# Another order of the attention's pieces in a list-scheduled decoder layer

## The chip, the core and the metric

The kernel runs on one core of a Trainium2 chip. The metric is the device time of one execution in microseconds (us), the median of three runs: 1217.39 us (1216.54, 1217.39 and 1219.12). One further execution was taken with the hardware profiler on. Engines are called PE (TensorE, the matrix products), PEld (its weight loads), DVE (VectorE), ACT (ScalarE), POOL (GpSimd) and SP (SyncE, which here only issues transfers).

## The reference

One layer of a decoder on a prompt of 1024 tokens and, beside it, 8 samples of one token each, with the same weights; the model is 1024 wide. All 1032 tokens go through the same products as columns.

```python
x = x + jnp.concatenate([ya, yb], axis=-1) @ w_out      # pooling and convolution mixers
x = x + cross_attn(rmsnorm(x, g_attn), mk, mv, w_q, w_o)
x = x + (jax.nn.silu(h @ w_gate) * (h @ w_up)) @ w_down # h = rmsnorm(x, g_ffn)

def cross_attn(h, k, v, w_q, w_o):                      # 4 heads of 256, 256 memory tokens
    q = (h @ w_q).reshape(B, L, MEM_HEADS, MEM_HEAD_DIM)
    s = jnp.einsum('blhd,bmhd->bhlm', q, k).astype(jnp.float32) / math.sqrt(MEM_HEAD_DIM)
    p = jax.nn.softmax(s, axis=-1).astype(v.dtype)
    o = jnp.einsum('bhlm,bmhd->blhd', p, v).reshape(B, L, D_MODEL)
    return o @ w_o
```

The prompt attends to one memory, whose keys and values (k, v) are computed here and shared by all its 1024 tokens. Each of the 8 samples has its own cached keys and values (2 MB of keys and 2 MB of values per head, for all samples), so its scores and values are not matrix products for PE; they are computed on DVE.

## The kernel before

Activations lie transposed: 128 channels on the partitions, tokens in the free dimension. A product of full precision is made of three passes over numbers split in two parts (high by high, high by low, low by high). A group of outputs, 128 channels by 1032 tokens, takes 72 matmuls of 344 columns (three spans, eight blocks of input, three passes). ACT copies a result to its high part, DVE subtracts to get the low part; that pair is called a drain here, and it frees the PSUM buffer that PE wants for a later group.

The attention is made of pieces, each a small function that adds tasks:

- `q` (`q_group`, line 1012): the queries of 128 channels, named `qo0` to `qo7`; two of them make a head. Their weights `w_q` come in two parts. For some groups the low part is made by DVE (line 384), for others ACT prepares it and a transfer from the POOL queue adds to it (line 402); which group of the order gets which is fixed by its place in the order.
- `S` (`scores`, line 1019): scores of a head for 256 tokens, 12 matmuls into `sc`, the maxima on DVE (1044), the exponentials on ACT (1053), the normalisation on DVE or POOL (1061). Pieces 0 to 3 are head 0, and so on; `sc3_1` is head 3, piece 1.
- `T` (`p_transpose`, line 1065): four transposes of the probabilities into `pt`, drained into `pT`.
- `P` (`pv`, line 1083): the values' products of 128 channels of a head, two halves of 512 tokens with 6 matmuls each, into `pv`, drained into `oo` by ACT (1098) and DVE (1099). Pieces 6 and 7 are head 3.
- For the samples of head h: `a` turns the queries into rows and writes them to memory (`qd`); `b` reads them back broadcast over the partitions (`sbcache_k`), loads the cached keys (`spcache_k`) and multiplies and sums on DVE (line 1133), four samples or eight at a time; `c` is their softmax (`ss`, `sst`, `prow`), written to `pd`; `d` does with the values (`sbcache_v`, `spcache_v`) what `b` did with the keys; `e` (POOL, lines 375 and 384) splits the result into the sample columns of `oo`.
- `o` (`proj_o`, line 1194): a group of the output product, `po`, over all `oo`. For `o0` and `o4` the columns with the samples come last. Its x (`x1d`) is loaded into `xa`, the sum is written to `x2d`. The pieces from `x` on (lines 1231 to 1247 are theirs) prepare the feed-forward part.

The table `ORDER` (line 41) lists the pieces; lines 1618 and 1619 run through it. That does not fix the order of instructions by itself: it numbers the tasks. `Program.order` (line 146) then plays the tasks through with costs written down in the kernel and picks for each engine the task that can start first, within a small slack the one with the lowest number. Buffers have slots: `pv`, `ps` and `po` share two (of three PSUM banks each), small tiles like `pt`, `ss` and most `sc` share two of one bank, the samples' cache tiles share three or, where eight samples go at once, lie among the operands' slots. A task whose buffer has no free slot waits. An engine executes its instructions in the order that comes out, and so does each queue of transfers, SP's and POOL's.

Of the kernel before, what the change touches and what calls it, by code (L numbers as in the profile page):

```python
# [40 lines left out]
ORDER = (  # L41
# [5 lines left out]
)  # L47

# [27 lines left out]
A12, A22, S4, S1, A11, S2, S3 = range(7)  # L76
# [1786 lines left out]
```

## Time and profile before

| | us |
|---|---|
| median of three runs | 1217.39 |
| lowest, highest | 1216.54, 1219.12 |
| the profiled execution's own time | 1217.88 |
| its span in the profile | 1216.1 |
| PE busy in it | 1198.4 |
| last query group's products end, the next scores begin | 409.78 |
| first output product (`po`) begins | 447.82 |

A row of the timeline reads: start, length, engine, line, operation, output and inputs by name, how often; in brackets how long the engine was idle before it, and on which instruction it waited. Names in the profile have lost their numbers, so `pv` is any of the eight. PE's lengths overlap, since the next matmuls start while the last ones run out. A row of the windows names, for a stretch of the span, the busy time and instruction count of each engine, the granted clock of PE (1.00 is full speed), the share of time that the transfer engines were busy, and their rate. In an answer on one tile, "DMA to landing" is the time from the issue of its transfers until a semaphore tells that they have landed, for those where the trace shows it.

### The profile page before, as it was taken

Reading aid. Unit: us, or ns where it says so; the run is one execution under the profiler, and the core shown is the slowest. Engines: PE = TensorE matmul, PEld = TensorE weight load, DVE = VectorE, ACT = ScalarE, POOL = GpSimd, SP = SyncE. Lnnn points to the kernel's source line nnn. Section 1 sums busy time; section 2 is a strip of 40 time slices with the busy share of each in tenths; the row PEclk is TensorE's granted clock in tenths of the full one; section 3 lists DMA queues with packets and bytes.
Section 4 is the critical chain, followed back from the end, with each engine's and each line's share of the span. In section 5 each row is a group of like instructions: output and inputs, shape, how many; then the busy total and the mean of one; then the engine's idle time right before and its main releaser. Section 6 shows DMA issues by size and latency. Waiting matters only on the chain.

```text
span 1216.1 us, 19401 instructions
## 1 busy us (share of the span) xinstructions
PE 1198.4 (99%) x7720; PEld 1121.8 (92%) x7720; DVE 930.1 (76%) x1548; ACT 524.7 (43%) x718; POOL 251.4 (21%) x297
## 2 busy tenths in 40 slices
PE   8999999999999999999999999999999999999997
PEld 7999988999999979999999999999999999999886
DVE  7999999766258886679877777777867798879744
ACT  7765656455135533454222322233222355544633
POOL 3568842231111102131000000000000024332101
PEclk9999999999999999999999999999999999999999
DMA  7335677326386774422332233222313597678612
GB/s 289 86 73 116 144 210 223 117 104 207 108 266 205 244 271 150 122 87 66 118 114 80 96 114 111 108 79 97 123 70 105 206 309 216 169 195 222 150 52 89
DMA packets 60170, 179.69 MB, mean 148 GB/s; under 512 B 7792, under 2 KB 11568, under 8 KB 58800
## 3 DMA queue, kind: packets, MB, share of 16 engines
q1 hardware_dynamic: 53824, 157.92, 37.4%
q0 software_dynamic: 6256, 20.54, 9.9%
q8 instruction: 60, 0.98, 0.3%
q14 instruction: 30, 0.25, 0.1%
HBM read 144.66 MB, written 33.78 MB: 147 GB/s over the span
## 4 chain that ended last, share of the span: by engine, by line
PE 78%; DVE 4%; DMA 1%; issue 1%; ACT 1%; POOL 0%; DVEq 0%; SPq 0%; ACTq 0%
PE pr L1339 48%; PE po L485 8%; PE fd L1682 6%; PE ps L485 5%; PE oa L485 4%; PE ob L485 4%; PE sc L1036 1%; DVE spcache_k L1133 1%; PE pv L1094 1%; DMA sbcache_v<-pd 1%; DVE oo L1099 1%; PE kps L860 0%; DVE pT L1080 0%; DMA raw<-in_w_k 0%; DMA pd<-prow 0%
## 5 line engine op out<-in xcount | busy, mean ns | idle before, releaser
L1339 PEld LDWEIGHTS pr<-ab,wTb 128*128 128x128 f32 x1056 | 131.8, 188 | 3.5
L1339 PE MATMUL pr<-ab,wTa 128*128 128x260 f32 x1056 | 133.6, 282 | 0.2 <-DVE su L1355 0.2
L1339 PE MATMUL pr<-ab,wTb 128*128 128x260 f32 x1056 | 133.0, 282 | 0.0
L1339 PEld LDWEIGHTS pr<-ab,wTa 128*128 128x128 f32 x1056 | 130.8, 188 | 2.4 <-DVE su L1355 0.4
L1339 PE MATMUL pr<-ab,wG 128*128 128x512 f32 x528 | 129.3, 393 | 0.0
L1355 DVE TENSOR_TENSOR su<-pr,su 128x520 f32<-128x520 f32 (+1 forms) x112 | 77.7, 695 | 57.9 <-PE pr L1339 57.7
L1339 PEld LDWEIGHTS pr<-ab,wG 128*128 128x128 f32 x528 | 96.3, 188 | 19.7 <-DVE wG L384 0.4
L485 PE MATMUL ps<-xop,w 128*128 128x344 f32 x720 | 114.1, 320 | 0.0
L485 PEld LDWEIGHTS ps<-xop,w 128*128 128x128 f32 x720 | 113.6, 188 | 0.0
L1339 PEld LDWEIGHTS pr<-hb,dV 128*128 128x128 f32 x768 | 98.8, 188 | 4.1
L1339 PE MATMUL pr<-hb,dV 128*128 128x260 f32 x768 | 100.1, 283 | 0.0
L485 PE MATMUL ps<-xq,w 128*128 128x344 f32 x576 | 94.9, 322 | 0.5 <-DMA w<-in_w_q 0.5
L485 PEld LDWEIGHTS ps<-xq,w 128*128 128x128 f32 x576 | 90.8, 188 | 0.9 <-DMA w<-in_w_q 0.8
L485 PEld LDWEIGHTS po<-oo,w 128*128 128x128 f32 x576 | 90.8, 188 | 0.6 <-DVE oo L1099 0.4
L485 PE MATMUL po<-oo,w 128*128 128x344 f32 x576 | 91.3, 320 | 0.0
L694 DVE SCALAR_TENSOR_TENSOR cacc<-glu,vec,cacc 128x511 f32<-128x511 f32 (+14 forms) x116 | 76.9, 744 | 0.0
L1339 PE MATMUL pr<-hb,dW 128*128 128x512 f32 x288 | 74.6, 394 | 0.0
L373 ACT ACTIVATE w<-raw 128x1024 fp32r<-128x1024 f32 (+1 forms) x37 | 34.9, 949 | 86.1 <-PE po L485 24.2
L1682 PE MATMUL fd<-ho,w 128*128 128x260 f32 (+1 forms) x432 | 69.1, 321 | 0.0
L1366 POOL MEMSET su<- 128x16 f32 x22 | 2.5, 112 | 318.9 <-PE pr L1339 267.7
L1682 PEld LDWEIGHTS fd<-ho,w 128*128 128x128 f32 x432 | 62.0, 188 | 6.9 <-issue 0.5
L1339 PE MATMUL pr<-ab,wU 128*128 128x512 f32 x264 | 64.6, 393 | 0.0
(309 smaller groups left out, 2189.2 us busy)
## 6 DMA issues: line engine op xcount, KB each, us to landing
gr<-in_w_gu SPq DMA_DIRECT2D x44, 512.0 KB, 3.7
hb<-su SPq DMA_DIRECT2D x8, 1040.0 KB, 4.6
hs<-hb SPq DMA_DIRECT2D x16, 520.0 KB, 5.1
dr<-in_w_dn SPq DMA_DIRECT2D x16, 512.0 KB, 4.6
spcache_k<-in_cache_k SPq DMA_DIRECT2D x12, 512.0 KB, 5.1
hs<-hb SPq DMA_DIRECT2D x12, 512.0 KB, 5.0
raw<-in_w_in SPq DMA_DIRECT2D x10, 512.0 KB, 3.7
hb<-he SPq DMA_DIRECT2D x8, 520.0 KB, 3.6
```

The costliest lines, as they stand in the source:

```text
L373: e.activation(dst(0), src(), AF.Copy, scale=1.0 if gain is None else gain)
L485: e.matmul(ps[:, c, :CW], w[:, wi, cols], x[:, xi, c * CW : (c + 1) * CW], start=first and p == 0, stop=last and p == 2)
L694: e.scalar_tensor_tensor(acc[h][:, n:], src[:, : HALF - n], w, acc[h][:, n:], ALU.mult, ALU.add)
L1036: e.matmul(bank()[:, i * NMEM : (i + 1) * NMEM], qop[2 * h + dt][:, qi, tt * P : (tt + 1) * P], kk[:, ki, 2 * (h % 2) + dt], start=(dt == ...
L1094: e.matmul(ps[:, c], v[:, vi, m, col : col + P], pT[h][m][:, pi, sl], start=(m == 0 and p == 0), stop=(m == 1 and p == 2))
L1099: add({"DVE": dve(512)}, lambda e, c=c, sl=sl: e.tensor_tensor(oo[:, 1, sl], ps[:, c], f32(oo[:, 0, sl]), ALU.subtract), [(ps, c), (oo, 0, ...
L1133: e.scalar_tensor_tensor(piece[:, b], piece[:, b], 1.0, bc[:, b], ALU.mult, ALU.mult, accum_out=out(m)[:, first + b : first + b + 1])
L1339: e.matmul(bank(c), w[:, wi, cols(j)], xs[0](j, xi)[:, c * n : (c + 1) * n], start=onto is None and j == 0 and p == 0, stop=j == nj - 1 an ...
L1355: from_sums(sums, "DVE", dve, lambda e, src, sl: e.tensor_tensor(as_banks(o(sl), src), src, as_banks(a(sl), src), op), [akey], [okey])
L1366: add({"Pool": 0.12}, lambda e: e.memset(o(), 0.0), [], keys)
L1682: e.matmul(view(i), w[:, wi, col : col + P], hops[k][:, xi, half, lo - half * HALF + i * width // count : lo - half * HALF + (i + 1) * wid ...
```

## The change

Two lines of the table are written anew, from the pieces behind `q5` to the last one ahead of `o0`. The pieces are the same.

```diff
--- before.py
+++ after.py
@@ -41,8 +41,8 @@
 ORDER = (
     "m5 A3 n0 g1 v1 g2 v2 m3 m7 m4 C0 g3 v3 C1 m0 s1 s0 A2 m1 D0 A0 m2 m6 A1 K0 K1 V1 W3 D1 W0 K2 s3 s2 W1 W2 C2 M0 M3 V0 "
     "C3 D2 D3 M1 L0 M2 K3 O0 O1 O3 O2 B0 t0 t1 B1 t2 t3 B2 t4 t5 B3 t6 t7 q0 q1 Z0 a0 b0 f0 q2 c0 q3 a1 b1 c1 S4 S0 S6 S5 "
-    "S2 q4 q5 a2 Y0 S7 S1 S3 S8 T0 d0 T3 T4 S9 T1 S10 T2 d1 q6 T8 q7 S11 T11 T5 P1 S12 T10 a3 S15 S13 T9 S14 T12 b2 T7 T6 "
-    "T13 b3 T14 T15 c3 c2 d2 P4 e1 e0 P5 P2 P3 P7 d3 P0 e3 P6 e2 o0 u0 o4 o1 o5 x1 u4 u1 u5 h0 x0 x4 y0 o2 z0 x5 h2 h3 u2 "
+    "S2 q4 q5 S1 S7 a2 S3 S8 S10 T0 T3 S9 T4 q7 T2 T1 T8 Y0 q6 d0 d1 S11 P1 S12 T11 e0 S15 S13 T5 b2 a3 S14 T6 b3 T9 T10 "
+    "T12 T7 c3 c2 d2 P5 P2 d3 T14 P0 T13 P4 e1 P3 T15 e3 e2 P7 P6 o0 u0 o4 o1 o5 x1 u4 u1 u5 h0 x0 x4 y0 o2 z0 x5 h2 h3 u2 "
     "o6 u6 o3 u3 y1 z1 o7 x2 y2 x3 h1 i0 y3 x6 z2 u7 r0 i1 x7 j0 j1 z3"
 )
 
```

`q7` now comes ahead of `q6`, with its weight prepared in the way that fell to `q6` before and the reverse. The second, third and later scores of heads 1 and 2 come earlier, the transposes of heads 0 to 3 in other turns. The values' products, which stood as `P1` early and `P4 P5 P2 P3 P7 P0 P6` near the end, now stand as `P1` and `P5 P2 P0 P4 P3 P7 P6`, with the samples' pieces `d2`, `d3`, `e1`, `e2`, `e3` and two transposes between them. What the scheduler makes of this differs between 361 us and the first output products. Three places are shown, those that the prediction speaks of.

The first is DVE behind the last scores: where the samples' key products of head 3 (`spcache_k3`), the drains of `pv` (L1099) and those of the transposes (L1080) stand. Before:

```order
L1099 TENSOR_TENSOR oo4_4216<-pv4_4175,oo4_4216 128x512 x2
L1080 TENSOR_TENSOR pT3_0_4200<-pt3_1_4219,pT3_0_4200 128x512
L1133 SCALAR_TENSOR_TENSOR spcache_k3_0_0_4009,ssc_81<-spcache_k3_0_0_4009,sbcache_k3_0_4158 128x256 x4
L1133 SCALAR_TENSOR_TENSOR spcache_k3_1_0_4012,ssc_81<-spcache_k3_1_0_4012,sbcache_k3_0_4158 128x256 x4
L1080 TENSOR_TENSOR pT3_1_4251<-pt3_2_4236,pT3_1_4251 128x512
L1080 TENSOR_TENSOR pT3_1_4251<-pt3_3_4253,pT3_1_4251 128x512
L1099 TENSOR_TENSOR oo5_4258<-pv5_4225,oo5_4258 128x512 x2
L1154 TENSOR_REDUCE sst2_4301<-ss2_4289 8x1
L1155 SCALAR_TENSOR_TENSOR sst2_4301<-sst2_4301,r16_79 8x1
L1099 TENSOR_TENSOR oo2_4161<-pv2_4266,oo2_4161 128x512 x2
L1162 RECIPROCAL sst2_4301<-sst2_4301 8x1
L1163 TENSOR_SCALAR prow2_4305<-prow2_4305,sst2_4301 8x256
```

and now:

```order
L1099 TENSOR_TENSOR oo5_4205<-pv5_4173,oo5_4205 128x512 x2
L1080 TENSOR_TENSOR pT3_0_4224<-pt3_0_4210,pT3_0_4224 128x512
L1133 SCALAR_TENSOR_TENSOR spcache_k3_0_0_4013,ssc_81<-spcache_k3_0_0_4013,sbcache_k3_0_4168 128x256 x4
L1133 SCALAR_TENSOR_TENSOR spcache_k3_1_0_4015,ssc_81<-spcache_k3_1_0_4015,sbcache_k3_0_4168 128x256 x4
L1154 TENSOR_REDUCE sst2_4263<-ss2_4239 8x1
L1155 SCALAR_TENSOR_TENSOR sst2_4263<-sst2_4263,r16_79 8x1
L1099 TENSOR_TENSOR oo2_4170<-pv2_4216,oo2_4170 128x512 x2
L1099 TENSOR_TENSOR oo0_3977<-pv0_4242,oo0_3977 128x512
L1162 RECIPROCAL sst2_4263<-sst2_4263 8x1
L1163 TENSOR_SCALAR prow2_4271<-prow2_4271,sst2_4263 8x256
L1099 TENSOR_TENSOR oo0_3977<-pv0_4242,oo0_3977 128x512
L1080 TENSOR_TENSOR pT3_1_4290<-pt3_2_4276,pT3_1_4290 128x512
```

The first eight products stood ahead of the drain of `pv5` and now stand behind it, ahead of that of `pv2`. Transfers on SP at the same place, before:

```order
L359 DMA sbcache_k3_0_4158<-qd_86 128x1024
L359 DMA sbcache_k3_4_4264<-qd_86 128x1024
L359 DMA spcache_k3_0_4_4276<-in_cache_k 128x1024
L359 DMA spcache_k3_1_4_4284<-in_cache_k 128x1024
L359 DMA pd_87<-prow2_4305 8x256
L359 DMA spcache_v3_0_0_4329<-in_cache_v 128x2048
L359 DMA spcache_v3_1_0_4332<-in_cache_v 128x2048
L359 DMA sbcache_v2_0_4347<-pd_87 128x2048
```

and now (`spcache_v3`, 1 MB each, are the cached values of head 3, `xa` the x of the output product):

```order
L359 DMA sbcache_k3_0_4168<-qd_86 128x1024
L359 DMA spcache_v3_0_0_4201<-in_cache_v 128x2048
L359 DMA sbcache_k3_4_4254<-qd_86 128x1024
L359 DMA spcache_k3_0_4_4266<-in_cache_k 128x1024
L359 DMA spcache_k3_1_4_4269<-in_cache_k 128x1024
L359 DMA spcache_v3_1_0_4273<-in_cache_v 128x2048
L359 DMA pd_87<-prow2_4271 8x256
L359 DMA xa0_4339<-x1d_82 128x1032 x2
L359 DMA xa1_4354<-x1d_82 128x1032
L359 DMA sbcache_v2_0_4359<-pd_87 128x2048
```

The values of head 3 moved ahead of the second broadcast and right behind the second pair of keys, and loads of `xa` ahead of the broadcast of head 2.

The second is PE at the end of the attention. Before:

```order
L1146 MATMUL ss3_4349<-ident_74,ssc_81 8x128 x2
L1094 MATMUL pv0_4354<-pT0_0_3773,vv0_2016 128x512 x3
L1094 MATMUL pv0_4354<-pT0_1_3796,vv0_2016 128x512 x3
L1094 MATMUL pv0_4354<-pT0_0_3773,vv0_2016 128x512 x3
L1094 MATMUL pv0_4354<-pT0_1_3796,vv0_2016 128x512 x3
L1094 MATMUL pv6_4379<-pT3_0_4200,vv1_1805 128x512 x3
L1094 MATMUL pv6_4379<-pT3_1_4251,vv1_1805 128x512 x3
L1094 MATMUL pv6_4379<-pT3_0_4200,vv1_1805 128x512 x3
L1094 MATMUL pv6_4379<-pT3_1_4251,vv1_1805 128x512 x3
L485 MATMUL po0_4403<-oo0_4208,w44_3820 128x344 x6
```

and now:

```order
L1146 MATMUL ss3_4341<-ident_74,ssc_81 8x128 x2
L1075 MATMUL pt3_3_4346<-ident_74,probs3_4094 128x128 x4
L1094 MATMUL pv7_4361<-pT3_0_4224,vv1_1805 128x512 x3
L1094 MATMUL pv7_4361<-pT3_1_4290,vv1_1805 128x512 x3
L1094 MATMUL pv6_4374<-pT3_0_4224,vv1_1805 128x512 x3
L1094 MATMUL pv6_4374<-pT3_1_4290,vv1_1805 128x512 x3
L1094 MATMUL pv7_4361<-pT3_0_4224,vv1_1805 128x512 x3
L1094 MATMUL pv7_4361<-pT3_1_4290,vv1_1805 128x512 x3
L1094 MATMUL pv6_4374<-pT3_0_4224,vv1_1805 128x512 x3
L1094 MATMUL pv6_4374<-pT3_1_4290,vv1_1805 128x512 x3
L485 MATMUL po0_4404<-oo0_3977,w44_3835 128x344 x6
```

`pv7` and `pv6` now come in alternating halves, straight ahead of `po0`, and the last transpose of head 3 stands behind its samples' softmax; `pv0` went forward.

The third is POOL around the weight of the fourth output group (`w47`, whose low part the transfer of line 402 completes). Before:

```order
L384 TENSOR_TENSOR w46_4584<-raw46_3621,w46_4584 128x1024
L375 TENSOR_SCALAR ab4_0_4622<-xa0_4386,vec_68 128x512
L375 TENSOR_SCALAR ab0_0_4626<-xa0_4386,vec_68 128x512
L402 DMA w47_4606<-in_w_o 128x1024
L384 TENSOR_TENSOR ab6_0_4709<-xa0_4386,ab6_0_4709 128x520
```

and now:

```order
L384 TENSOR_TENSOR w46_4575<-raw46_3587,w46_4575 128x1024
L1232 TENSOR_SCALAR xa0_4339<-xa0_4339,vec_68 128x520
L375 TENSOR_SCALAR ab0_0_4638<-xa0_4339,vec_68 128x512
L402 DMA w47_4621<-in_w_o 128x1024
L384 TENSOR_TENSOR ab6_0_4700<-xa0_4339,ab6_0_4700 128x520
```

A scaling of `xa0` (line 1232), which overwrites it and so waits until it has been written to `x2d`, now stands ahead of that transfer.

## The prediction

> **What bounds the kernel now.** I read the page first: the busy time of each engine.
>
> ```profile
> span 1216.1 us, 19401 instructions
> PE 1198.4 (99%) x7720; PEld 1121.8 (92%) x7720; DVE 930.1 (76%) x1548; ACT 524.7 (43%) x718; POOL 251.4 (21%) x297
> ```
>
> TensorE (PE) is busy for 1198.4 of 1216.1 us, so the whole span holds under 18 us that an order could give back. The question is how much of it lies where the table changes, and what a worse order could add. The changed pieces run from about 361 us (the score piece that follows q5) to about 448 us, where `o0` begins. The windows of that stretch (length, then busy us and instructions of PE, PE's weight loads, DVE, ACT and POOL, the granted clock, the DMA share and GB/s):
>
> ```profile
> 360.00:380.00 20.00, 19.88 (x142) 19.45 (x141) 18.80 (x83) 9.12 (x26) 3.40 (x4) 1.00 0.75 217
> 380.00:400.00 20.00, 20.00 (x146) 19.93 (x145) 16.98 (x59) 11.07 (x27) 1.73 (x4) 1.00 0.60 202
> 411.00:422.00 11.00, 10.67 (x77) 9.38 (x76) 9.30 (x22) 8.63 (x22) 1.71 (x5) 1.00 0.88 269
> 422.00:433.00 11.00, 10.89 (x63) 8.95 (x63) 9.70 (x32) 7.88 (x19) 0.40 (x2) 1.00 0.34 135
> 433.00:448.00 15.00, 13.62 (x59) 10.14 (x58) 12.31 (x38) 5.76 (x13) 0.00 (x0) 1.00 0.89 326
> 448.00:480.00 32.00, 32.00 (x203) 31.85 (x204) 18.82 (x73) 8.24 (x10) 6.43 (x12) 1.00 0.67 241
> ```
>
> Up to 400 us PE is idle for 0.12 us: the query products cover everything there. It is the last part, after the last query group, that loses time, at full granted clock (1.00). There VectorE (DVE) is busy for 9.70 of 11 and 12.31 of 15 us. From 448 us on PE is full again. Now PE itself in that tail, from its timeline (start, length, in brackets the idle time before and its releaser; overlapping lengths, so I count from start to start):
>
> ```profile
> 409.78 1.58 PE L1036 MATMUL sc<-kT,qo 128*128 128x256 f32 x12
> 411.20 2.94 PE L1094 MATMUL pv<-pT,vv 128*128 128x512 f32 x12
> 413.98 0.60 PE L1075 MATMUL pt<-ident,probs 128*128 128x128 f32 x4
> ...
> 427.28 0.60 PE L1075 MATMUL pt<-ident,probs 128*128 128x128 f32 x4
> 427.63 1.65 PE L1094 MATMUL pv<-pT,vv 128*128 128x512 f32 x6
> ...
> 435.70 5.84 PE L1094 MATMUL pv<-pT,vv 128*128 128x512 f32 x24 [1.15 <-DVE oo L1099]
> 441.37 0.38 PE L1146 MATMUL ss<-ident,ssc 128*8 128x128 f32 x2
> 441.99 5.83 PE L1094 MATMUL pv<-pT,vv 128*128 128x512 f32 x24 [0.23 <-DVE oo L1099]
> 447.82 36.38 PE L485 MATMUL po<-oo,w 128*128 128x344 f32 x228
> ```
>
> The tail runs from 409.78 to 447.82, 38.04 us. Its work, start to start: a score piece 1.42, a values' product pv of 12 matmuls 2.78, a transpose 0.35. It holds 5 scores (7.1), 10 transposes (3.5), 8 pv (22.2) and three small pairs for the samples (an estimate of 0.15 each from the 0.62 between 441.37 and 441.99 less its wait): 33.3 us. So 4.7 us of the tail are idle or gaps between groups. That is the most that any order of the tail can give back: 0.39% of the time.
>
> **The change part by part.**
>
> *Nothing is added or removed in matmuls.* Each engine's order holds the same products. What is new in kind: the split of one w_o weight goes from ACT and DVE to POOL, long before its use, and more of the score normalisations (L1061) run on POOL. Cost on PE nothing, as long as other PE work covers them.
>
> *Before 409.78 (q7 ahead of q6, scores and K products of the samples moved).* The same number of scores and transposes stands ahead of the last query group in both orders, so the work is equal. The cover is the query groups, with only 0.12 us idle; the gain is at most 0.1. What can be lost: DVE is busy for 18.80 of 20 us at 360 to 380, and the weight split that now stands between two sets of four of its sample products delays the scores' maxima behind it. Such a split takes 1.2 us (the w row in the last fence), the bounds are −0.1 and +1.2, and I take 0, since PE has matmuls of a query group to do between these scores and the transposes that read them.
>
> *The tail.* Up to the end of pv5 the orders differ by a transpose here and there; I carry the idle over: from 427.63 on the old order holds six pv (16.7), two transposes and two pairs, 17.7 in 20.19 us, so 2.5 of the 4.7 lie there and 2.2 ahead of it. The rest depends on DVE, which drains each pv (ACT copies, DVE subtracts) and also computes the samples' K products of the last head, L1133. Its rows now:
>
> ```profile
> 428.60 1.29 DVE L1099 TENSOR_TENSOR oo<-pv,oo 128x512 fp32r<-128x512 f32 x2 [1.19 <-ACT oo L1098]
> 429.80 0.68 DVE L1080 TENSOR_TENSOR pT<-pt,pT 128x512 fp32r<-128x512 f32 x1
> 430.40 0.42 DVE L1133 SCALAR_TENSOR_TENSOR spcache_k<-spcache_k,sbcache_k 128x256 f32<-128x256 f32 x1
> ...
> 433.16 1.29 DVE L1080 TENSOR_TENSOR pT<-pt,pT 128x512 fp32r<-128x512 f32 x2
> 434.36 1.28 DVE L1099 TENSOR_TENSOR oo<-pv,oo 128x512 fp32r<-128x512 f32 x2
> 435.56 0.40 DVE L1154 TENSOR_REDUCE sst<-ss 8x1 f32<-8x256 f32 x1
> 436.07 1.27 DVE L1099 TENSOR_TENSOR oo<-pv,oo 128x512 fp32r<-128x512 f32 x2
> ...
> 437.87 0.43 DVE L1133 SCALAR_TENSOR_TENSOR spcache_k<-spcache_k,sbcache_k 128x256 f32<-128x256 f32 x1
> ```
>
> Eight products take 2.76 (430.40 to 433.16), a pair of drains or transposes 1.20, the small sst pair 0.51. The 1.15 wait of PE at 435.70 is the drain that ended at 435.6, late because eight products stood ahead of it. In the new order that drain (oo5) goes ahead of the products, but the next one (oo2) stands behind them: the wait moves from pv3 to pv4. I count from the end of pv5 (zero). DVE: oo5 until 2.0 (ACT's copy ends 0.8 after the matmuls), one transpose 2.6, eight products 5.4, sst 5.9, oo2 7.1. PE: transpose, pv2, ss2, pv0, transpose: ready for pv4 at 6.4 to 6.7, and oo2's buffer is free at 7.1. Wait 0.5 to 1.3 (the upper end if the products start 0.7 later, as in the row of 1.19 above); I take 0.7. The 1.15 before is thereby not won.
>
> Then pv4 to 10.1, transpose, pv3 to 13.2. DVE meanwhile: oo0 with the samples' row between its halves 8.9, transpose 9.5, four products 10.9, half of oo4 11.5, four products 12.9, transpose 13.5. So ss3, which needs the second products, is just not late at 13.2, and the last transpose waits 0.2 for its buffer. Behind it sst3 and the other half of oo4, which frees the buffer that pv7 wants: 14.7, when PE stands ready at 13.9. A wait of 0.8. The end is pv7 and pv6 in alternating halves: 14.8, 16.2, 17.6, 19.0, 20.4; each half finds the other's drain just done (0.1 to 0.2 twice). How long a drain takes at the end, the rows show:
>
> ```profile
> 445.08 0.60 ACT L1098 ACTIVATE oo<-pv 128x512 fp32r<-128x512 f32 x1 [1.91 <-PE pv L1094]
> 446.44 0.60 ACT L1098 ACTIVATE oo<-pv 128x512 fp32r<-128x512 f32 x1 [0.76 <-DVE oo L1099]
> ```
>
> From the end of a half to its drained half is 0.2 and 0.6 (ACT) and 0.6 (DVE), against 1.39 for the half between. `po0` starts at 20.6 to 20.8; its work from zero is six pv 16.7, four transposes 1.4, two ss 0.3: 18.4. Idle 2.2 to 2.4 with no gaps counted, 2.3 to 2.9 with them, against 4.7 − 2.2 = 2.5 before: −0.2 to +0.4.
>
> The Trainium skill (Perfetto Trace Analysis, Optimizing Tensor Performance, Matmuls) says that independent groups should rotate through different PSUM banks, so that one's evacuation lies beside the next one's matmuls. By that rule the alternating halves of pv7 and pv6 cost nothing, 0.3 less than my sum; the trace before, where ACT waits 0.76 for DVE between the halves of one drain, has no alternating halves to settle it.
>
> *The loads.* SP now issues the 1 MB V cache loads of the last head around the K loads that the second four products want, instead of at 438 us. The rows:
>
> ```profile
> 422.52 9.69 SPq L359 DMA_DIRECT2D sbcache_k<-qd  x2
> 433.27 0.81 SPq L359 DMA_DIRECT2D spcache_k<-in_cache_k  x2
> 438.21 0.81 SPq L359 DMA_DIRECT2D spcache_v<-in_cache_v  x2
> L359 SPq DMA_DIRECT2D spcache_v<-in_cache_v x2: 338/380/423, 438.2 to 438.6; - x2
> DMA to landing us min/median/max: 4.9/4.9/4.9
> ```
>
> The second broadcast of the queries goes out at 431.9, 1.5 after the first product, the K pair 2.9 after it, and DVE found the first K tile landed at 437.87, 7.5 after the first product, and the second four products later. In the new order the products start at 2.6 and the second K tiles are wanted at 9.5 and 11.5, that is 6.9 and 8.9 after the first product: up to 0.6 late, if they landed only just in time before. One V load of 1 MB goes ahead of the broadcast, into a stretch where the DMA share is 0.34; the other goes right behind the pair. The first of two 1 MB loads issued 0.4 us apart landed after 4.9, although the other stood right behind it: a follower did not hold up its predecessor. I take 0.1 of the 0 to 0.6.
>
> *The sum.* −0.2 to +0.4 in the tail (I take 0.1, nearer the middle), 0.1 for the K tiles, 0 before the tail, 0 behind it (third rival): 1217.88, the profiled execution's time, becomes 1218.1. That execution stands 0.49 above the median of 1217.39, so a median of 1217.6 is what the sum says; I give 1217.7. Faster or slower by 0.2% is 2.4 us, about what a measurement of this kernel can tell from no change.
>
> **The rivals.**
>
> 1. *The K pair lands late (slower).* If the 1 MB load behind it shares the transfer engines evenly, the pair of 1 MB needs up to twice its 4.6, and the second products start up to 9 − 4.6 = 4.4 later; ss3, both remaining drains and pv7 queue behind them on DVE. With 1 us of cover that is +3.3: 1221.0. It decides as soon as the pair lands 3.4 late. For it: the DMA share of 0.89 at 433 to 448. Against it: the 4.9 of the row above. The Trainium skill (DMA: Bandwidth & Descriptors, Queues, rings and completion order) says that each transfer engine consumes one queue's descriptors in ring order and goes round between queues. All these loads are SP's, so by that rule the pair is not held up; the 4.9 agrees.
>
> 2. *The spreading works (faster).* If the drains keep up as the order intends, the waits for buffers go: 1.15 and 0.23 and the gaps of the late part, 2.5 in all, at most 4.7 with the early part. 1215.2 for the median, at the very best 1212.7. For it: half-drains placed between products. Against it: the eight products still stand in one row ahead of oo2.
>
> 3. *The weight of the fourth output group is late.* On POOL its DMA now stands behind a scaling (L1232) that waits until x2 is written out. The rows:
>
> ```profile
> 468.04 1.23 DVE L1205 TENSOR_TENSOR xa<-po,xa 128x1032 f32<-128x1032 f32 x1 [5.19 <-PE po L485]
> 473.33 0.89 POOL L402 DMA_DIRECT2D w<-in_w_o  x1 [0.39 <-ACT w L395]
> DMA to landing us min/median/max: 8.1/8.1/8.1
> L1232 POOL TENSOR_SCALAR xa<-xa,vec x1: 1974/1974/1974, 543.2 to 543.2; 128x520 f32<-128x520 f32 x1
> L359 SPq DMA_DIRECT2D x2d<-xa x3: 319/327/382, 469.3 to 486.2; - x3
> DMA to landing us min/median/max: 6.3/6.3/6.3
> 489.01 0.73 ACT L1231 ACTIVATE xa<-xa,vec 128x520 f32<-128x520 f32 x1 [1.09 <-DMA x2d<-xa]
> 486.26 1.21 DVE L384 TENSOR_TENSOR w<-raw,w 128x1024 fp32r<-128x1024 f32 x1
> ```
>
> Now that DMA goes out at 473.3 and lands 8.1 later, at 481.4. PE reaches the group 216 matmuls after `po0`'s start, at 0.16 each (36.38 for 228) 482.6, and the weight's low half, which is what this DMA completes, about 0.7 later. In the new order `po0` ends after 114 matmuls instead of 126, so the first x2 (468.04 and 1.23) is there at 467.5. A write of it took 6.3 beside weight loads, but the one of 486.2, alone, let ACT go on at 489.0, after 2.8. Nothing else stands on the queues at 467.5, so I take 2.8: scaling 470.3 to 472.3, one POOL piece of 0.7, DMA at 473.0, landed 481.1. No wait. With 6.3 it lands at 484.6: +1.3, 1218.9.
>
> 4. *The stretch before 409.78 slips (slower).* Normalisations on POOL and the split on DVE make scores late: 1.2 once is 1218.9; if it recurs at each of the two remaining query groups, +3: 1220.7.
>
> **How the numbers follow.** Chances: my sum 0.50, rival 1 0.15, rival 2 0.15, rival 3 0.08, rival 4 0.12. Rival 3 and half of rival 4 end within 0.2%; my sum's own errors put 0.04 beyond the bound on the slow side and 0.02 on the fast one; of rival 2, 0.13 is beyond it. That makes faster 0.15, same 0.60, slower 0.25. The range must reach rival 1's 1221.0 and rival 2's 1215.2; a little beyond the latter, 1215.0 to 1221.0. The likeliest case alone spans 1216.8 to 1218.8.
>
> **What would show it.** In the changed kernel's trace PE's waits on "DVE oo" should total 1.5 to 2.5 us, the longest ahead of pv4, and `po` should start within 0.7 us of 447.8. Eight K products of 0.345 in one row ahead of oo2's drain would show the moved wait. Wrong would be: a wait of pv or ss for products that follow an spcache_k landing (rival 1); `po` before 446 (rival 2); a PE wait on a w_o weight near 483 (rival 3); the last query group ending after 411 (rival 4).

## The result and the profile after

The changed kernel takes 1220.18 us (median of 22 runs, 1217.84 to 1223.63), the kernel before beside it 1218.36 (22 runs, 1216.54 to 1220.75). The ratio is 1.0016, with a 95% interval of 1.0010 to 1.0022: 1.9 us more. That is under the 0.2% that the prediction takes as no change, but it is not zero, and on the slow side. The profiled execution took 1221.16 us with a span of 1219.4, 1.0 above the median; the profile of before was at 1217.88.

The windows of the changed kernel, with the same columns as before:

```profile
360.00:380.00 20.00, 19.94 (x144) 19.62 (x143) 16.87 (x73) 9.59 (x25) 3.52 (x5) 1.00 0.62 199
380.00:400.00 20.00, 20.00 (x148) 19.87 (x147) 17.38 (x62) 10.24 (x29) 7.08 (x10) 1.00 0.59 183
411.00:422.00 11.00, 10.81 (x80) 9.65 (x79) 9.59 (x26) 9.00 (x23) 2.21 (x5) 1.00 0.93 267
422.00:433.00 11.00, 10.58 (x54) 8.28 (x52) 8.04 (x29) 5.92 (x14) 1.57 (x4) 1.00 0.77 252
433.00:448.00 15.00, 12.47 (x49) 9.36 (x50) 12.14 (x39) 6.46 (x14) 0.12 (x1) 0.89 0.96 359
448.00:480.00 32.00, 32.00 (x199) 31.11 (x198) 19.37 (x73) 7.63 (x9) 6.69 (x12) 1.00 0.51 182
```

Up to 411 us nothing is lost. From 422 on PE is idle for 0.42 and 2.53 us (0.11 and 1.38 before), and in the window of 433 to 448 the granted clock is 0.89 instead of 1.00. PE's timeline of the tail:

```profile
409.20 1.58 PE L1036 MATMUL sc<-kT,qo 128*128 128x256 f32 x12
...
432.03 0.60 PE L1075 MATMUL pt<-ident,probs 128*128 128x128 f32 x4
434.82 4.41 PE L1094 MATMUL pv<-pT,vv 128*128 128x512 f32 x12 [2.19 <-DVE oo L1099]
439.03 0.84 PE L1075 MATMUL pt<-ident,probs 128*128 128x128 f32 x4
...
443.12 0.66 PE L1075 MATMUL pt<-ident,probs 128*128 128x128 f32 x4 [0.24 <-DVE pT L1080]
444.22 6.17 PE L1094 MATMUL pv<-pT,vv 128*128 128x512 f32 x24 [0.45 <-DVE oo L1099]
450.35 35.94 PE L485 MATMUL po<-oo,w 128*128 128x344 f32 x226
```

The tail is 41.15 us long instead of 38.04, and the last query group ends 0.58 earlier, so `po` starts 2.53 later. The wait of the moved drain is where the count put it, ahead of pv4, but 2.19 long. (The spans of the two profiles differ by 3.3 us; the 0.8 that the tail does not hold lie behind `po`, a stretch that takes 768.3 to 769.3 us in the profiles of all versions, old order and new.) And pv4 itself takes 4.21 us from start to start, where a pv took 2.78 before. The windows of PE alone say why (length, busy time, granted clock, DMA share, GB/s):

```profile
433.00:434.00 1.00, 0.00 (x0) 1.00 0.91 319
434.00:435.00 1.00, 0.18 (x1) 1.00 0.80 213
435.00:436.00 1.00, 1.00 (x5) 1.00 0.76 209
436.00:437.00 1.00, 1.00 (x5) 0.55 0.81 229
437.00:438.00 1.00, 1.00 (x4) 0.50 0.94 307
438.00:439.00 1.00, 1.00 (x3) 0.50 1.06 401
439.00:440.00 1.00, 1.00 (x7) 0.75 1.03 426
```

About 1.3 us after PE went back to work its clock was halved, for 0.9 + 1 + 1 + 0.5 = 3.4 us. Of the 3.11 us by which this tail is longer, 1.43 are pv4's, and the rest is in the main waiting. But the fall belongs to this execution more than to the kernel: each run lists its mean granted clock, and over its 22 runs the changed kernel has 0.9976, the kernel before 0.9975 over 35. One fall of 3.4 us at half takes some 0.0014 off that mean (1.7 of 1219). The mean is below 1 without any such fall, because in every profile the clock stands at 0.5 once more at the end of the span, behind PE's last matmul, where it costs nothing: for 4 to 7 us, worth 0.0016 to 0.0030. A run that lists 0.998 therefore has no room for a fall in the tail as well. Of the 22 runs of the changed kernel 15 list 0.998, and they average 1219.8; the 20 of the 35 of before that list it average 1218.2. So 1.6 us stand between runs that had no fall. The clock explains part of this profile, which stands 1.0 above the median, and little of the 1.9 us. DVE in the same stretch:

```profile
428.34 0.68 DVE L1080 TENSOR_TENSOR pT<-pt,pT 128x512 fp32r<-128x512 f32 x1
430.21 0.42 DVE L1133 SCALAR_TENSOR_TENSOR spcache_k<-spcache_k,sbcache_k 128x256 f32<-128x256 f32 x1 [1.19 <-DMA sbcache_k<-qd]
...
433.50 1.96 DVE L1099 TENSOR_TENSOR oo<-pv,oo 128x512 fp32r<-128x512 f32 x3
...
438.42 0.42 DVE L1133 SCALAR_TENSOR_TENSOR spcache_k<-spcache_k,sbcache_k 128x256 f32<-128x256 f32 x1 [1.33 <-DMA spcache_k<-in_cache_k]
```

Two landings came late: the broadcast of the queries by 1.19, and a K tile of the second pair by 1.33, 8.2 us after the first product. The broadcast took 7.0 us from its issue to its landing. For the same broadcast before, issued at 422.52, the trace shows no landing (the 3.4 us that it gives there are the second one's, issued at 431.9). It took 4.5 us at most, since the transfer engines moved nothing between 427.0 and 431.5. The tile came 5.3 us after its issue; before, DVE found it landed 4.6 after.

### The profile page after: what moved, and what is told of

The parts are those of the page before. It is cut to its first block, busy times and chain, and to the rows that moved or that the text cites. A ratio compares the mean times of both kernels' runs of the same rounds, so it can differ in the third digit from the quotient of the medians.

```text
span 1219.4 us, 19406 instructions
## 1 busy us (share of the span) xinstructions
PE 1199.9 (98%) x7720; PEld 1122.7 (92%) x7720; DVE 927.1 (76%) x1539; ACT 523.2 (43%) x717; POOL 258.3 (21%) x307
## 4 chain that ended last, share of the span: by engine, by line
PE 78%; DVE 3%; DMA 2%; ACT 1%; issue 1%; POOL 0%; DVEq 0%; SPq 0%; ACTq 0%; POOLq 0%
PE pr L1339 46%; PE po L485 7%; PE ps L485 7%; PE fd L1682 6%; PE oa L485 4%; PE ob L485 4%; PE sc L1036 1%; PE pv L1094 1%; DMA dr<-in_w_dn 1%; DMA sbcache_k<-qd 1%; PE kps L860 0%; DMA hs<-hb 0%; DVE spcache_k L1133 0%; DMA raw<-in_w_k 0%; DMA qd<-qrow 0%
```

## The experiments

Where instructions are moved without the scheduler, the list of tasks that it returns is taken and some tasks are put behind another; an engine's other instructions stay as they are.

```diff
-    for t, e in pg.order():
+    issued = pg.order()
+    def behind(group, mark):
+        took = [x for x in issued if group(*tag(*x))]      # tag: engine, is it a transfer, names of its buffers
+        rest = [x for x in issued if not group(*tag(*x))]
+        at = max(i for i, x in enumerate(rest) if mark(*tag(*x))) + 1
+        return rest[:at] + took + rest[at:]
```

The table gives for each the ratio to the kernel before, and from its profile the length of the tail (last query group to `po`) and the granted clock in 433 to 448 us.

| kernel | ratio (95%) | tail, us | clock |
|---|---|---|---|
| before | 1 | 38.04 | 1.00 |
| changed | 1.0016 (1.0010 to 1.0022) | 41.15 | 0.89 |
| e1, V loads late | 1.0017 (1.0008 to 1.0026) | 40.85 | 0.89 |
| e2, first V load late | 1.0017 (1.0005 to 1.0028) | 39.08 | 1.00 |
| e3, products behind the drain | 1.0051 (1.0039 to 1.0064) | 43.12 | 0.90 |
| e4, before with a longer wait | 1.0016 (1.0008 to 1.0025) | 40.51 | 0.89 |
| e5, e11, new early part alone | 1.0007 (0.9998 to 1.0016), 1.0002 (0.9993 to 1.0011) | 39.95, 38.90 | 1.00, 1.00 |
| e6, e12, new tail alone | 1.0007 (0.9998 to 1.0016), 1.0009 (0.9997 to 1.0021) | 40.79, 38.33 | 0.89, 1.00 |
| e7, before with split products | 1.0027 (1.0016 to 1.0038) | 40.33 | 1.00 |
| e8, before with a little more wait | one execution | 39.79 | 0.89 |
| e9, changed with short products | 1.0001 (0.9991 to 1.0011) | 37.14 | 1.00 |
| e10, before with products earlier | 1.0004 (0.9994 to 1.0014) | 37.59 | 1.00 |

**e1: the loads of head 3's values back where they were.**

```diff
+    issued = behind(lambda e, d, n: e == "SP" and d and n in (["spcache_v3_0_0"], ["spcache_v3_1_0"]),
+                    lambda e, d, n: e == "SP" and n == ["prow2"])
```

> The changed kernel with both 1 MB loads of head 3's cached values put back in SP's queue to the place they had before (behind the write of head 2's samples' softmax); all else in the new order. Theory (the early loads make the broadcast of the queries land late): the broadcast lands in about 3.5 us instead of 7.0, the first eight K products start near 429.0 instead of 430.2, the second four do not wait for their tile, PE's wait ahead of pv4 falls from 2.2 to about 1.0, PE's granted clock stays at 1.00 in 433 to 448, the first output product begins at 447.3 to 448.3, and the time is that of the kernel before, ratio 0.9990 to 1.0008. Rival (the order of the drains alone makes the wait): the wait stays at 1.8 or more, the clock falls as in the changed kernel, ratio 1.0012 to 1.0022.

Half of it came. (The 3.5 us expected were the second broadcast's, so the first could not be held to them.) The broadcast landed after 5.0 instead of 7.0 us, and PE's wait ahead of pv4 fell to 0.91. But the second four products waited for their tile all the same, 1.06 us, and the tail got no more than 0.3 shorter. PE's waits in this profile:

```profile
PE pv L1094 <- DVE oo L1099: 1.4, 2, 0.9
PE sc L1036 <- ACT probs L1053: 0.9, 1, 0.9
PE ss L1146 <- DVE spcache_k L1133: 0.9, 1, 0.9
PE pt L1075 <- DVE pT L1080: 0.3, 1, 0.3
```

Three short waits, 0.87, 0.33 and 0.45, now stand between 441 and 444 us, and in this profile the clock was halved behind them; the mean over all runs is 0.9976, that of the changed kernel. The time is the changed kernel's too, so the early loads are not what costs it: the theory fell here. The tile landed 5.4 us after its issue with no load behind it for 3 us, as late as with one (5.1 to 5.6 in e2, changed, e3 and e6; in e12, with one, it was there after 4.3 at most).

**e2: only the first of the two loads back.**

```diff
+    issued = behind(lambda e, d, n: e == "SP" and d and n == ["spcache_v3_0_0"], lambda e, d, n: e == "SP" and n == ["prow2"])
```

> The changed kernel with only the first of the two loads of head 3's cached values put back behind the write of head 2's softmax; the second stays right behind the second pair of keys. If the first load alone delays the broadcast, the wait ahead of pv4 is about 1.0 and the clock stays up, while the second four K products still wait about 1.3 for their tile, and the ratio is 1.0000 to 1.0010. If the load behind the pair is what counts, it stays near 1.0016 with the wait ahead of pv4 at 1.8 or more.

The wait ahead of pv4 is 0.91 again, ss3 waits 0.55, the clock stays up in this profile and the tail is 39.08. The ratio, 1.0017, is above the 1.0010 that was expected of the first load alone, and the rival had a wait of 1.8: neither holds. In all of these the broadcast's time shows no clear rule: 5.0 and 4.8 us without a 1 MB load right behind it (e1, e2), 7.0, 6.5, 5.0, 4.6 and 4.6 with one (changed, e6, e9, e3, e12). In the old order it took 4.5 at most before, but in e10 DVE waited for it until 5.2 us after its issue. What stands ahead of it in the queues must count too; that was not taken apart.

**e3: the drain ahead of the products.**

```diff
+    issued = behind(lambda e, d, n: "sbcache_k3_0" in n and e == "DVE" or e == "SP" and n in (["sbcache_k3_4"],
+                    ["spcache_k3_0_4"], ["spcache_k3_1_4"], ["spcache_v3_1_0"]), lambda e, d, n: e == "DVE" and n == ["oo2", "pv2"])
```

> The changed kernel with the eight K products of head 3 (and the loads that need their buffers) moved behind the drain of pv2 on DVE; the early loads stay. The wait ahead of pv4 falls under 0.5 us and the clock stays up until there. Theory (loads and products are late as a whole): what is saved there comes back at ss3, whose products end 1 to 2 us later, so PE waits 1 to 2.5 us ahead of the last transpose and pv7; ratio 1.0004 to 1.0016. Rival (the drain behind the products is the whole cause): no new wait, ratio 0.9985 to 1.0003.

The wait ahead of pv4 is gone, as expected, and what comes back at ss3 is more than expected:

```profile
437.20 3.06 PE L1094 MATMUL pv<-pT,vv 128*128 128x512 f32 x12 [0.24 <-DVE oo L1099]
442.67 0.27 PE L1146 MATMUL ss<-ident,ssc 128*8 128x128 f32 x1 [2.42 <-DVE spcache_k L1133]
444.56 0.27 PE L1146 MATMUL ss<-ident,ssc 128*8 128x128 f32 x1 [1.62 <-DVE spcache_k L1133]
```

The products free the buffers into which the second pair is loaded, so the later first eight delay the pair, the second eight, and ss3: the pair is issued 2.4 us later than in the changed kernel's profile, of which 1.1 are the later end of the last query group, and lands 5.5 after its issue. Here the clock does count: the mean over the five runs is 0.9954, 0.0021 below before, some 2.6 us by the rule above. Together the kernel loses 6 us. The rival, that the drain behind the products is the whole cause, fell: the products have a deadline of their own, on the other side.

**e9: the products made short.** The last test of where the loss sits.

```diff
+                            f = 32 if number == 3 else 256
-                            e.scalar_tensor_tensor(piece[:, b], piece[:, b], 1.0, bc[:, b], ALU.mult, ALU.mult,
+                            e.scalar_tensor_tensor(piece[:, b, :f], piece[:, b, :f], 1.0, bc[:, b, :f], ALU.mult, ALU.mult,
```

> The changed kernel with the 16 K products of head 3's samples taken over 32 of 256 columns (the other columns' part of these samples' scores is left out); their loads and their places stay. Theory (DVE's products stand ahead of the drains that PE waits for, and late loads only add to it): DVE is free some 4 us earlier in the tail, PE's wait ahead of pv4 falls to 0.2 to 0.8 although the first broadcast may still land at 430, ss3 and pv7 wait less than 0.5 together, the clock stays at 1.00, the tail takes 37 to 39 us; ratio 0.9985 to 1.0003. Rival (the landing of the loads is what counts): the waits at ss3 stay over 0.5 and the clock falls in the profile, ratio 1.0006 to 1.0018.

The loss is gone: 1.0001, and a tail of 37.14, although the broadcast landed as late as 429.3 and all loads are in their new places. One wait, 0.85 ahead of pv7, is left, where under 0.5 was expected; in the wait ahead of pv4 the expectation was too careful (none).

```profile
439.37 0.38 PE L1147 MATMUL ss<-ident,ssc 128*8 128x128 f32 x2
441.04 6.19 PE L1094 MATMUL pv<-pT,vv 128*128 128x512 f32 x24 [0.85 <-DVE oo L1099]
447.18 8.02 PE L485 MATMUL po<-oo,w 128*128 128x344 f32 x49
```

So the tail's loss passes through DVE's chain: first products, second loads, second products, ss3, with PE's drains queued between them. How much of the 1.9 us that is, e9 does not show. The same cut in the kernel before was not run, and it would shorten the row of products behind its wait of 1.15 too. Also, e9's tail is 0.9 shorter than that of before, and its time is not below that of before, so something outside the tail may cost part of the loss.

**e4 and e8: a longer wait in the kernel before.** In both the second half of pv5's drain is repeated, which changes no value; e8 does it twice, e4 three times.

```diff
-            add({"DVE": dve(512)}, lambda e, c=c, sl=sl: e.tensor_tensor(...),
+            add({"DVE": dve(512)}, lambda e, c=c, sl=sl: [e.tensor_tensor(...) for _ in range(3 if (n, c) == (5, 1) else 1)],
```

> The kernel before with the second half of pv5's drain on DVE (0.60 us, the same values) done three times, so that PE's wait ahead of pv3 grows from 1.15 by 1.2 to about 2.35 us. Theory (a wait of over 2 us makes the clock gate halve PE's clock for some 3.4 us): a granted clock of 0.5 for part of 436 to 441 and a time longer by 1.2 and 1.4 to 1.7, +2.6 to +2.9 us, ratio 1.0021 to 1.0024. Rival (the clock fell for another reason): clock 1.00 throughout, +1.2 us or less, ratio 1.0005 to 1.0010.

> The kernel before with the second half of pv5's drain done twice: PE's wait ahead of pv3 grows from 1.15 to about 1.75 us, its idle time there from 1.4 to about 2.0. If the clock falls only when more than some 2 us of about 3.4 are idle, as the four profiles so far have it (fallen at 2.2 to 2.8 us, not at 1.4 and 1.9), it stays at 1.00 and the time grows by 0.6 or less; if a gap of 1.75 is enough, a granted clock of 0.5 shows for part of the 5 us behind it.

Both halve the clock, and e4 does it in most executions: 9 of its 11 runs have a mean of 0.996, and none of them 0.998, which more than half of the runs of before have. In e4 the wait is 2.60, in e8 1.89; PE's rows of e8, and its clock behind the wait:

```profile
433.89 0.38 PE L1146 MATMUL ss<-ident,ssc 128*8 128x128 f32 x2
436.17 7.40 PE L1094 MATMUL pv<-pT,vv 128*128 128x512 f32 x24 [1.89 <-DVE oo L1099]
443.40 0.38 PE L1146 MATMUL ss<-ident,ssc 128*8 128x128 f32 x2
```

```profile
436.00:438.00 2.00, 1.83 (x6) 0.78 0.82 301
438.00:440.00 2.00, 2.00 (x6) 0.50 0.53 119
440.00:442.00 2.00, 2.00 (x9) 0.87 0.75 299
```

The 24 matmuls take 7.23 from start to start, 5.67 before: 1.56 for 0.74 us more of waiting. Counted from the rows, the halved time is 0.9 + 2.0 + 0.5 = 3.4 us, as in the changed kernel. The loss of e4, 1.9 us by the ratio, is less than the 2.6 to 2.9 expected: its tail grew by 2.47, of which 1.45 is the longer wait and most of the rest the clock, and the median lies below what one profile shows. e8 was to leave PE idle for 2.0 us, just under the point from which the clock was thought to fall. The wait came out at 1.89 instead of 1.75 and PE was idle for 2.1, so the fall neither contradicts that point nor confirms it. Another kernel, e7 below, shows that it is no fixed bound.

**e5, e6, e11, e12: the early part alone and the tail alone.** e5 and e11 are the new order up to `q6` with the old rest, e6 and e12 the old order up to `q7` with the new rest.

```diff
+e5, e11: S1 S7 a2 S3 S8 S10 T0 T3 S9 T4 q7 T2 T1 T8 Y0 q6 d0 d1 S11 T11 T5 P1 ... c2 d2 P4 e1 e0 P5 P2 P3 P7 d3 P0 e3 P6 e2 o0
+e6, e12: a2 Y0 S7 S1 S3 S8 T0 d0 T3 T4 S9 T1 S10 T2 d1 q6 T8 q7 S11 P1 S12 T11 ... c2 d2 P5 P2 d3 T14 P0 T13 P4 e1 P3 T15 e3 e2 P7 P6 o0
```

> The new order up to the piece q6 (q7 ahead of q6, scores of heads 1 and 2 earlier, more normalisations on POOL), then the old one: the tail with the values' products as before. Theory (only the tail's order costs): the last query group ends within 0.7 us of the kernel before when counted from the start of the group of q6's and q7's neighbour q5, the tail takes 38 us as before, the clock stays at 1.00 in 433 to 448, ratio 0.9993 to 1.0007. Rival (the early part makes scores and loads late): ratio 1.0010 or more with the last query group late by 1 us or more.

> The old order up to q7, then the new one: the new tail alone. Theory: the tail takes 40 to 41.5 us as in the changed kernel, with PE's wait ahead of pv4 at 0.9 to 2.2, further waits of 1 to 2 us at the last sample softmax and ahead of pv7, and a fall of the clock if the idle time in some 3.4 us is over 2 us; ratio 1.0008 to 1.0024. Rival (the early part is needed for the loss): tail 38 us, ratio 0.9993 to 1.0006.

> The new order up to q6 with the old tail, once more, since its first 11 runs leave open (0.9998 to 1.0016) how the 1.6 per thousand of the whole change is shared. In its profile a pair of K loads of head 2 landed 8.6 to 9.2 us after its issue, and a score waited 1.8 us behind them. If that belongs to the new early order, such a wait shows again and the ratio is again 1.0005 to 1.0010; if it was one execution's, there is none and the ratio is 0.9996 to 1.0004.

> The old order up to q7 with the new tail, once more, for the same reason. Theory (the new tail costs the most): tail of 39 to 41 us with waits ahead of pv4, at ss3 and ahead of pv7, ratio 1.0008 to 1.0018. Rival (it costs half or less): ratio 1.0000 to 1.0007.

All four intervals hold 1.0000, and 1.0016 is in them or just beyond; the early part's two are 1.0007 and 1.0002, the tail's 1.0007 and 1.0009. How the 1.6 per thousand divides is not settled by them. The profiles tell more. In e5 a score waited 1.8 us, which its tail of 39.95 holds, and that was one execution's: a K pair of head 2 landed 9.2 us after its issue, and e11 has no such wait. But in e11, with the old tail, a K tile of the second pair of head 3 came 0.88 late, 5.4 us after its issue and 8.3 after the first product; PE then waited 0.93 ahead of the last pv instead of 0.23. So a late tile is not the new tail's alone. Of the tail alone the two profiles show both of its ways. e12's is short:

```profile
433.38 3.01 PE L1094 MATMUL pv<-pT,vv 128*128 128x512 f32 x12 [0.91 <-DVE oo L1099]
...
440.27 0.66 PE L1075 MATMUL pt<-ident,probs 128*128 128x128 f32 x4 [0.33 <-DVE pT L1080]
441.37 6.17 PE L1094 MATMUL pv<-pT,vv 128*128 128x512 f32 x24 [0.45 <-DVE oo L1099]
```

The broadcast landed after 4.6 us and DVE waited for no landing. The waits are 0.91, 0.33 and 0.45, ss3 has none, and the tail of 38.33 is 0.3 longer than before. In e6, the same program, the second K tile was 1.3 late, ss3 waited 1.07, the clock fell behind the three waits that followed each other, and the tail was 40.79. The medians of e6 and e12, 1218.23 and 1218.25, are within 0.2 of the kernel before (1218.04 and 1218.15), and their longest runs reach 1222.51 and 1224.82. Taken together, the 22 runs of the tail alone average 0.9 us more than the 35 of before (0.1 to 1.9 when the runs are drawn anew many times), the 22 of the early part 0.5 (−0.1 to 1.0). So the new tail costs something in a part of its executions; for the early part that is not shown.

**e7 and e10: the kernel before with other places for its products.** e7 puts four of the eight behind pv5's drain, e10 four ahead of pv4's drain.

```diff
+e7:  issued = behind(lambda e, d, n: e == "DVE" and n == ["sbcache_k3_0", "spcache_k3_1_0"] or e == "SP" and n in
+         (["sbcache_k3_4"], ["spcache_k3_1_4"]), lambda e, d, n: e == "DVE" and n == ["oo5", "pv5"])
+e10: the task of ["sbcache_k3_0", "spcache_k3_0_0"] on DVE goes right ahead of the first of ["oo4", "pv4"] on DVE
```

> The kernel before with only four of the eight K products of head 3 ahead of pv5's drain on DVE and four behind it; the second broadcast and the second of the pair of keys go out behind them. If the wait of 1.15 ahead of pv3 is bought back without a new one, the time falls by 1.0 to 1.4 us, ratio 0.9988 to 0.9992. If the second products then become the end of DVE's chain, as in the changed kernel, ss3 waits 0.5 to 1.5 us and the ratio is 0.9996 to 1.0008.

> The kernel before with the first four of the eight K products of head 3 moved ahead of pv4's drain on DVE, into the 1.2 us in which DVE waits there for ACT. Expected from DVE's rows: pv5's drain ends 1.2 earlier, PE's wait of 1.15 ahead of pv3 falls to 0.0 to 0.3, the second products start about 1 us earlier, and the first output product with them: 0.8 to 1.4 us less, ratio 0.9988 to 0.9994. Against it: if the queries' broadcast lands later than 427.4 in most executions, DVE waits for it ahead of pv4's drain, and the gain is gone or turns: 0.9996 to 1.0010.

e7 is slower, by more than the upper bound of its second case: the wait ahead of pv3 is gone, ss3 waits 0.30 and 1.73 for the second products, and the last pv 0.93.

```profile
440.64 0.27 PE L1146 MATMUL ss<-ident,ssc 128*8 128x128 f32 x1 [0.30 <-DVE spcache_k L1133]
442.64 0.27 PE L1146 MATMUL ss<-ident,ssc 128*8 128x128 f32 x1 [1.73 <-DVE spcache_k L1133]
443.84 2.36 PE L1094 MATMUL pv<-pT,vv 128*128 128x512 f32 x9 [0.93 <-DVE oo L1099]
```

```profile
440.00:442.00 2.00, 0.61 (x3) 1.00 0.96 368
442.00:444.00 2.00, 0.43 (x2) 1.00 1.03 430
444.00:446.00 2.00, 2.00 (x9) 1.00 0.99 418
446.00:448.00 2.00, 2.00 (x10) 1.00 1.00 417
```

PE is idle for 3.0 of 4 us, more than in e8, and the clock stays at 1.00 in this execution. In others of the same kernel it fell: its runs have means from 0.994 to 0.998, 0.9966 over all. e10 does in its profile what was expected of it in part: no wait is left ahead of pv3, 0.51 ahead of pv0, a tail of 37.59, 0.45 less than before. But DVE waited 0.49 for the broadcast, which landed at 428.1, later than the 427.4 that the expectation names against it. Its ratio, 1.0004 (0.9994 to 1.0014), shows no gain. No version here beats the kernel before.

## Why the prediction was right, and where it was off

*The bound and the place* held. PE's work is the same, the stretch before the tail gave and took nothing in the changed kernel's profile (the last query group ended at 409.20, 0.58 earlier), and that profile's difference sits mostly in the tail, its longest wait on the drain that was named. The signs that the prediction asked for were missed there: the waits on "DVE oo" are 2.64 us in all instead of 1.5 to 2.5, and `po` starts 2.5 late instead of within 0.7.

*The tail's sum*, 0.1 for a range of −0.2 to +0.4, holds when loads land as they did in the old order: e12's profile gives +0.29, with the waits 0.91 (forecast 0.5 to 1.3), 0.33 (0.2) and 0.45 (0.8). The 0.3 counted for the alternating halves of pv7 and pv6 came too: 6.13 us from their start to `po`, and 6.14 in e12, against 5.83 for the last two pv before. *The step that was too small* is the one on the loads, "I take 0.1 of the 0 to 0.6". It treated the K tiles of the second four products alone, took the first broadcast as landed when DVE came to it, and set the latest landing at 7.5 us after the first product, although that row shows no wait and so only when DVE came to the tile. In the changed kernel the broadcast was 1.19 late and the tile 1.33, 8.2 us after the first product. The count had left DVE's products no cover: first products, second loads, second products and ss3 follow each other with about 0.3 us to spare. A landing that comes 1 us later is paid by PE almost in full (0.70 for 0.88 in e11), and e9, which takes about 4 us of DVE's work from this chain, brings the time back.

*What the forecast did not ask* is the clock. It read 1.00 in the windows of before and went no further. In the profiled execution of the changed kernel pv4 took 4.21 instead of 2.78, 1.4 of the 3.1 us by which its tail is longer, and in e8 0.74 us more of waiting came with 1.56 of slower matmuls. Over all executions it is at most a small term of this change's 1.9 us, since the mean clocks are the same and the runs without a fall differ by 1.6; it is one of e4's and e3's.

*Rival 1* (the load behind the pair holds it up) has its signs in the profiles, late landings and waits behind the products (at ss3 in e1, e2 and e6), but not its cause: with both loads taken away (e1) the ratio stays at 1.0017 and the tile is as late. *Rival 2* came nowhere: the eight products ahead of oo2 made the wait, as said against it; its two times were counted from two starts, 1215.2 from 1217.7 and 1212.7 from 1217.39. *Rival 3* did not come. Its steps in the changed kernel:

```profile
472.87 0.71 POOL L1232 TENSOR_SCALAR xa<-xa,vec 128x520 f32<-128x520 f32 x1 [0.67 <-DMA x2d<-xa]
475.82 0.89 POOL L402 DMA_DIRECT2D w<-in_w_o  x1 [0.42 <-ACT w L395]
```

The write of x2, issued at 469.91, let POOL go on 2.96 later (2.8 had been taken), the scaling took 0.71 and not 1.97, and the weight was there at 483.7, before PE, now at 484.9. *Rival 4* was not seen in the changed kernel; the early part alone measured 0.2 to 0.7 per thousand, not clear of zero.

The forecast median of 1217.7 stood 0.3 above the kernel before; measured are 1.8 above it (1220.18 against 1218.36 in the same runs; 1.9 by the ratio). That this lies in the range is in part luck: no change was right within 0.2%, but the sum had a sixth of the loss, and the range was wide on that side for rival 1, whose cause did not hold. What is shown: the loss goes when DVE's products are short; it does not go when the early loads are taken away; and it is there at an unchanged mean clock. What stays open: which transfers make the broadcast and the tile late, and how much of the loss belongs to the early part, which alone is not distinguishable from nothing and yet the new tail without it measured half of the whole. That late landings make the loss in the other executions too is argued from these profiles, not shown.

## What to carry to other kernels

When a chain runs through two engines and a queue (products, the loads into the buffers that they free, products again), count its slack from end to end, with the latest landing that any row shows and not the one that happened at this place: an order with 0.3 us of slack is as fast as the old one in one execution and some us slower in another (e12 and e6, 1217.89 and 1222.51 for one program, with 2.5 us of that in the tail). Moving work behind a drain to save a wait pays only if nothing waits for that work. And read the granted clock of every run, not only of the one that was profiled: here the profile's fall was real and still not the cause of the difference. A mean over the whole run also holds stretches in which a low clock costs nothing, here the one behind the last matmul.

## What the runs showed of the clock

PE's granted clock halved behind little more than 2 us of idle time. It fell behind single gaps of 2.1 us (e8), 2.4 (the changed kernel) and 2.8 (e4), counted from the end of one group's work to the next start, and in e1 behind three short waits that left PE idle for about 2.2 of 2.7 us. It stayed at 1.00 behind 1.4 (before), 1.9 of 2.4 (e2), 2.0 (e5) and, in one execution, 3.0 of 4 us (e7, by the busy time in its windows; its other executions show falls). Each fall stood at 0.5 for about 3.4 us, and the matmuls in that time cost 1.4 to 1.6 us more. So there is no fixed bound in these rows: the same idle time may cost nothing or 1.5 us. The Trainium skill (TensorE: Matmul & The Clock Gate, Part 1) describes a window of about 3.4 us that runs freely, whose activity sets the clock to full or half. The length of the falls and the two values agree with the rows, and a gap that two windows share would explain e7; where the windows lie no trace here shows. The Trainium skill's advice to keep idle gaps under some 3 us (same page, Why this matters for your kernels) is too generous for these kernels: 2.1 were enough.
